# Hybrid attention layer: differential query and key projections accumulated side by side, with their weights loaded tile by tile

## Chip, cores and metric

The kernel runs on one core of a Trainium2 chip, in one launch. The metric is the device time of one execution in microseconds (us); lower is better. The times are medians over repeated executions.

## The reference

One layer (DEPTH 1) on x of 256 tokens by 1024 features, all float32. One input projection feeds two attention branches; cut to what matters:

```python
h = rms_norm(x, norm_g)
proj = einsum('bsd,de->bse', h, w_in)          # 1024 -> 4096, eight chunks of 512
mq, mk, mv, mg, dq, dk, dv, dg = split(proj)
# branch m: 8 heads of 64, causal softmax attention with ALiBi, all 256 keys in one block
mq, mk = rms_norm(mq, moba_q_norm), rms_norm(mk, moba_k_norm)
m_out = moba_attention(mq, mk, mv) * silu(mg)
# branch d: 4 heads, two softmax maps each
dq, dk = rms_norm(dq, diff_q_norm), rms_norm(dk, diff_k_norm)
a = softmax(q1 k1) - lam * softmax(q2 k2)
d_out = rms_norm(a @ dv, diff_subln) * 0.8 * silu(dg)
x = x + einsum('bse,ed->bsd', concat([m_out, d_out]), w_out)
```

## The kernel before

**The projections.** Every float32 product is made of three reduced-precision matmuls: each operand is split in a rounded part "hi" and the rest "lo", and hi·hi, hi·lo and lo·hi are accumulated (`PASSES`). x stands transposed in eight k tiles of 128 rows (`xhi`, `xlo`); the weights are split into `whi` and `wlo` in pieces of 1024 columns, two k tiles of one chunk each. A step `u.n` is one *unit*: one k tile (n % 8) of chunk n // 8 in the order of `CHUNKS` (dq, dk, dv, mq, mk, mv, dg, mg), which is six matmuls of 512 columns (three products for each of two token tiles). So `u.0` to `u.7` are dq, `u.8` to `u.15` are dk. Units from `u.64` on are the output projection.

**Splitting.** hi is a copy on ACT (ScalarE), lo a subtraction on DVE (VectorE). `x.k` splits x and dq's weights of k tile k (they come in one DMA, tile `first`); `h.i` and `l.i` make `whi` and `wlo` of piece i, from weight tiles `w` of 1 MB (two pieces each, step `L.j` loads tile j). Tile j lands in one of three buffers, the split pieces in one of six.

**Between the projections.** `sq`, `ssq`, `norm`, `sc` compute and apply the RMS factors of queries and keys (ACT and DVE). `T.dq`, `T.dk` transpose them on TensorE (PE), `Th` and `Tl` split them again (ACT, DVE). `S.d` are the scores of branch d, `post.dv` copies the values out of PSUM, `rcopy` copies a row of factors. `X`, `E`, `C` are the softmax (DVE, ACT, DVE or POOL), `AT`, `AC`, `AV` transpose the probabilities, copy them and multiply by the values. `gds`, `gdi`, `gdm` are the gate of branch d (ACT sigmoid, DVE, POOL), after which `T.d` transposes its output. Steps ending in m do the same for branch m.

**What sets the order.** The table `ORDER` is written out by hand: the program issues its steps one after another, so each engine runs its own instructions in the order of the table, and waits in place for what it needs. PSUM has eight banks, handed out by a first-in-first-out list (`bank`, `release`): a step can also wait for the reader of the bank that it is given. All loads and stores are issued by SP (SyncE) in table order; the loads of `small`, and of `first` for all eight k tiles, stand ahead of the table. The first tile comes in two halves, and the first unit works on halves of 256 columns.

**Warm-up.** `warm_up(N_WARM)` issues seven matmuls on zeros ahead of the first unit, `warm_up(N_FILL)` two more behind it. Each leaves two matmul records in the profile.

Of the kernel before, what the change touches and what calls it, by code (L numbers as in the profile page):

```python
# [22 lines left out]
MAGIC = float(0x5F1FFFF9)  # L23
N1, N2 = 0.703952253, 0.703952253 * 2.38924456
LAMBDA_INIT = 0.2
N_WARM, N_FILL, N_TILES = 7, 2, 9
OUT_ORDER = "dm"
CHUNKS = ["dq", "dk", "dv", "mq", "mk", "mv", "dg", "mg"]
GAIN = {"mq": 8, "mk": 9, "dq": 10, "dk": 11, "subln": 12}
# [5 lines left out]


ORDER = """
x.0 x.1 x.2 x.3 x.4 L.0 L.1 LX L.2 LL x.5 x.6 x.7 u.0 u.1 u.2 h.4 u.3 l.4 u.4 u.5 h.5 l.5 L.3 u.6 u.7 h.6 l.6 u.8
sq.dq h.7 u.9 ssq.dq l.7 L.4 xsq xst u.10 u.11 h.8 l.8 u.12 lsum u.13 rdiag u.14 h.9 l.9 L.5 u.15 lexp ldiff u.16
sq.dk ssq.dk h.10 h.11 l.10 norm.d l.11 L.6 u.17 sc.dq sc.dk u.18 u.19 rmm u.20 u.21 T.dq h.12 l.12 h.13 h.14 l.14  # L40
T.dk Th.dk Tl.dk l.13 L.7 u.22 Th.dq u.23 post.dv h.15 rcopy u.24 Tl.dq u.25 l.15 L.8 S.d X.d0 E.d0 u.26 X.d1 E.d1
X.d2 u.27 E.d2 X.d3 E.d3 u.28 C.d1 C.d0 u.29 h.16 l.16 u.30 C.d2 u.31 sq.mq h.17 l.17 L.9 AT.d0 AC.d0 u.32 C.d3
h.18 l.18 h.19 l.19 h.20 l.20 L.10 u.33 ssq.mq AV.d0 u.34 h.21 l.21 u.35 u.36 AT.d1 AC.d1 L.11 u.37 u.38 AV.d1
u.39 h.22 l.22 u.40 u.41 h.23 l.23 L.12 h.24 l.24 u.42 u.43 sq.mk ssq.mk sqd norm.m sc.mq sc.mk normd u.44 T.mk
Th.mk Tl.mk scd u.45 T.mq u.46 Th.mq Tl.mq h.25 l.25 L.13 u.47 post.mv u.48 h.26 h.27 l.26 l.27 h.28 L.14 u.49 S.m
h.29 u.50 u.51 X.m0 E.m0 l.28 u.52 C.m0 X.m1 X.m2 E.m1 C.m1 X.m3 u.53 h.30 l.29 L.15 u.54 E.m2 C.m2 E.m3 C.m3
AT.m0 AC.m0 u.55 gds l.30 u.56 gdi h.31 l.31 gdm L.16 u.57 u.58 AT.m1 AC.m1 AT.m2 AC.m2 u.59 h.32 l.32 h.33 u.60
T.d l.33 AT.m3 L.17 u.61 Th.d Tl.d h.34 u.62 AV.m2 AV.m1 AV.m0 l.34 AC.m3 AV.m3 u.63 gi.0 gi.1 h.35 u.64 l.35 u.65
u.66 gs.1 u.67 u.68 gs.0 u.69 u.70 gm.1 gh.1 gl.1 u.71 gm.0 gh.0 gl.0 h.36 l.36 h.37 l.37 u.72 h.38 l.38 h.39 l.39
u.73 u.74 u.75 u.79  # L50
""".split()


# [1 line left out]
def kernel(  # L55
# [45 lines left out]
    small = const.tile([P, 16 + S], F32, name="small")  # L101
    nc.sync.dma_start(out=small, in_=small_x)
    sm = small[:, 0:16]
    first = []
    for kt in range(KT):
        t = tile768("first")
        if kt == 0:
            for c in (slice(S, 512), slice(512, 768)):
                nc.sync.dma_start(out=t[:, c], in_=xw[kt][:, c])
        else:  # L110
            nc.sync.dma_start(out=t, in_=xw[kt])
        first.append(t)
    xn = const.tile([P, 2, D], F32, name="xn")

    def load_xn():
# [123 lines left out]
                                       op0=ALU.subtract, op1=ALU.subtract)  # L239


    raws, pieces = {}, {}

    def load_w(i):
        t = raw_pool.tile([P, 2048], F32, tag="raw", name=f"w{i}")
        n = 2 if i < 2 else 1
        for j in range(n):
            c = slice(j * 2048 // n, (j + 1) * 2048 // n)
            nc.sync.dma_start(out=t[:, c], in_=w[i][:, c])
        raws[i] = t  # L250
# [29 lines left out]
    def unit_nat(name, kt, piece):  # L280

        if kt == 0:
            acc[name] = [bank(f"acc_{name}{t}") for t in range(2)]
        wp = pieces[piece]
        n = 256 if name == CHUNKS[0] and kt == 0 else 512
        order = [(t, i, o) for t in range(2) for i in range(3) for o in range(0, 512, n)]
        if name == CHUNKS[0]:
            order.sort(key=lambda v: (v[2], (0, 2, 1)[v[1]]))
        for t, i, o in order:
            a, b = PASSES[i]  # L290
            c = (kt % 2) * 512 + o
# [321 lines left out]
    def unit_out(u, piece):  # L613
# [79 lines left out]
```

## Time and profile before

| | |
|---|---|
| time, median of 3 runs (lowest to highest) | 143.33 us (143.05 to 143.37) |
| time of the profiled execution | 143.47 us |
| its span on the core | 141.7 us |
| PE matmul busy | 137.4 us, 97% |
| DVE / ACT / POOL busy | 105.8 / 84.2 / 23.7 us |
| moved by DMA | 24.39 MB, mean 172 GB/s |

The span is what the profile covers; the 1.8 us between it and the time lie outside. Busy shares are means over stages with different limits, so the question is where PE waits, not how busy the others are. An instruction's printed length on PE is the time until its result is through the array; a stream of matmuls is counted by the distance between starts.

### The profile page before, as it was taken

To read this page: it belongs to the slowest core of one execution; us is meant where nothing else is said; L and a number is where in the kernel's file an instruction comes from. 1 tells how busy PE (TensorE), PEld (TensorE's weight loads), DVE (VectorE), ACT (ScalarE), POOL (GpSimd) and SP (SyncE) were. 2 spreads that over 40 slices of the span, in tenths; PEclk is the share of its full clock that TensorE was granted. 3 is DMA by queue.
4 is the path that set the end of the run, shared out by engine and by line. 5 is a ranking of instruction groups with operands and counts; after the bars stand their busy time and mean duration, and the time that the engine had idled before them with its cause. 6 is when DMAs were issued, how large, how long until landed. Compare 5 with 4: busy or idle time off the path is not lost.

```text
span 141.7 us, 2227 instructions
## 1 busy us (share of the span) xinstructions
PE 137.4 (97%) x806; PEld 116.8 (82%) x806; DVE 105.8 (75%) x249; ACT 84.2 (59%) x167; POOL 23.7 (17%) x28
## 2 busy tenths in 40 slices
PE   7999999999999999999999999999999999999990
PEld 7888878888888888888887888878999888898890
DVE  1699996889995998997799999994629435691331
ACT  4477894495192898955650599799768504660000
POOL 7980000000000000000000000279750007000000
PEclk9999999999999999999999999999999999999999
DMA  4999999670708700068960002925134900000232
GB/s 111 307 408 381 418 430 407 250 273 25 296 0 296 298 2 0 9 287 291 335 268 0 0 0 93 416 88 213 83 113 187 296 0 0 7 0 0 104 118 74
DMA packets 5482, 24.39 MB, mean 172 GB/s; under 512 B 608, under 2 KB 1376, under 8 KB 3424
## 3 DMA queue, kind: packets, MB, share of 16 engines
q1 hardware_dynamic: 5472, 24.26, 46.1%
q8 instruction: 6, 0.10, 0.3%
q14 instruction: 4, 0.03, 0.1%
HBM read 23.21 MB, written 1.05 MB: 171 GB/s over the span
## 4 chain that ended last, share of the span: by engine, by line
PE 94%; DMA 3%; SPq 1%; DVE 0%; ACT 0%; issue 0%
PE oacc L601 16%; PE acc_mg L307 8%; PE acc_mq L292 8%; PE acc_dg L292 8%; PE acc_mk L292 8%; PE acc_dv L292 8%; PE acc_mv L292 8%; PE acc_dk L292 8%; PE acc_dq L292 8%; PE s_ps L412 4%; PE T_ps L317 3%; DMA first<-xw 3%; PE mo_ps L494 2%; PE do_ps L500 1%; PE aT_ps L470 1%; PE aT_ps L472 1%
## 5 line engine op out<-in xcount | busy, mean ns | idle before, releaser
L276 DVE TENSOR_TENSOR wlo<-w,whi 128x1024 fp32r<-128x1024 f32 x36 | 43.3, 1231 | 6.1 <-ACT whi L272 5.9
L272 ACT ACTIVATE whi<-w 128x1024 fp32r<-128x1024 f32 x36 | 36.4, 1056 | 4.1 <-DVE nq L175 2.1
L442 POOL TENSOR_TENSOR p<-p,rs 128x512 f32<-128x512 f32 (+1 forms) x8 | 8.3, 1064 | 82.0 <-DVE rs L438 81.8
L432 ACT ACTIVATE p<-p,nmax 128x256 f32<-128x256 f32 (+1 forms) x32 | 14.1, 442 | 3.9 <-DVE nmax L422 3.9
L601 PE MATMUL oacc<-whi,mixm 128*128 128x512 f32 (+1 forms) x40 | 10.4, 347 | 0.0
L601 PE MATMUL oacc<-whi,mixd 128*128 128x512 f32 (+1 forms) x40 | 10.4, 346 | 0.0
L422 DVE CUSTOM_DVE_ANT_0 p<-s_ps,bias 128x256 f32<-128x256 f32 (+1 forms) x32 | 9.2, 352 | 1.6 <-PE s_ps L412 1.5
L307 PE MATMUL acc_mg<-xhi,whi 128*128 128x256 f32 x32 | 9.2, 289 | 0.0
L307 PE MATMUL acc_mg<-xhi,wlo 128*128 128x256 f32 x32 | 9.0, 281 | 0.0
L307 PE MATMUL acc_mg<-xlo,whi 128*128 128x256 f32 x32 | 9.0, 281 | 0.0
L608 DVE TENSOR_TENSOR o<-oacc,xn 128x512 f32<-128x512 f32 (+1 forms) x5 | 2.9, 585 | 7.7 <-PE oacc L601 7.7
L601 PEld LDWEIGHTS oacc<-whi,mixm 128*128 128x128 f32 x40 | 7.1, 189 | 1.0
L601 PEld LDWEIGHTS oacc<-whi,mixd 128*128 128x128 f32 x40 | 7.0, 188 | 1.0
L143 POOL TENSOR_SCALAR bias<-dist 128x256 f32<-128x256 f32 x8 | 7.6, 967 | 0.4
L264 ACT ACTIVATE whi<-first 128x512 fp32r<-128x512 f32 (+1 forms) x9 | 5.0, 578 | 3.5 <-DMA first<-xw 3.5
L601 PE MATMUL oacc<-wlo,mixd 128*128 128x512 f32 (+1 forms) x20 | 6.9, 347 | 0.0
L601 PE MATMUL oacc<-wlo,mixm 128*128 128x512 f32 (+1 forms) x20 | 6.9, 347 | 0.0
L265 DVE TENSOR_TENSOR wlo<-first,whi 128x512 fp32r<-128x512 f32 (+1 forms) x9 | 6.0, 663 | 1.2 <-ACT whi L264 1.2
L478 ACT ACTIVATE pT<-aT_ps 128x512 f32<-128x512 f32 x6 | 3.6, 593 | 5.4 <-PE aT_ps L471 5.4
L292 PE MATMUL acc_mk<-whi,xhi 128*128 128x512 f32 x16 | 6.7, 418 | 0.0
L292 PE MATMUL acc_dv<-whi,xhi 128*128 128x512 f32 x16 | 6.5, 408 | 0.0
L292 PE MATMUL acc_mv<-whi,xhi 128*128 128x512 f32 x16 | 6.5, 405 | 0.0
(167 smaller groups left out, 353.9 us busy)
## 6 DMA issues: line engine op xcount, KB each, us to landing
w<-w SPq DMA_DIRECT2D x16, 1024.0 KB, 4.9
first<-xw SPq DMA_DIRECT2D x7, 384.0 KB, 5.6
w<-w SPq DMA_DIRECT2D x4, 512.0 KB, 8.6
xn<-x SPq DMA_DIRECT2D x2, 512.0 KB, 9.6
out<-o SPq DMA_DIRECT2D x3, 256.0 KB, 2.1
first<-xw SPq DMA_DIRECT2D x2, 128.0 KB, 3.0
out<-o SPq DMA_DIRECT2D x2, 128.0 KB, 1.9
small<-small_x SPq DMA_DIRECT2D x1, 136.0 KB, 2.2
```

What stands on the lines that cost most here:

```text
L143: nc.gpsimd.tensor_scalar(out=b, in0=dist, scalar1=2.0 ** -(h + 1), scalar2=None, op0=ALU.mult)
L264: nc.scalar.activation(out=hi[:, c], in_=src, func=AF.Copy)
L265: nc.vector.tensor_tensor(out=lo[:, c], in0=src, in1=hi[:, c].bitcast(F32), op=ALU.subtract)
L272: nc.scalar.activation(out=piece(i)[0], in_=raw_half(i), func=AF.Copy)
L276: nc.vector.tensor_tensor(out=lo, in0=raw_half(i), in1=hi.bitcast(F32), op=ALU.subtract)
L292: nc.tensor.matmul(acc[name][t][:, o:o + n], lhsT=(xhi, xlo)[a][:, kt, t * P:(t + 1) * P], rhs=wp[b][:, c:c + n], start=kt == 0 and i == 0 ...
L307: nc.tensor.matmul(acc[name][j // 2][:, (j % 2) * S:(j % 2 + 1) * S], lhsT=wp[b][:, c:c + P], rhs=(xhi, xlo)[a][:, kt], start=kt == 0 and ...
L412: nc.tensor.matmul(ps[c][k][:, o:o + n], lhsT=qk[g + "q"][a][rows, pr, q0:q0 + P], rhs=qk[g + "k"][b][rows, pr, 0:n], start=i == 0, stop=i ...
L422: nc.vector.tensor_tensor_reduce(out=p[:, o:o + n], in0=s_ps[g][c][k][:, b:b + n], in1=biases[c][:, S - n:], scale=-1.0, scalar=3.0e38, op ...
L432: nc.scalar.activation(out=p[:, o:o + n], in_=p[:, o:o + n], func=AF.Exp, scale=-1.0, bias=mx[:, i:i + 1], accum_out=sums[g, pr][:, i:i + 1])
L442: nc.gpsimd.tensor_tensor(out=p3, in0=p3, in1=q.unsqueeze(2).to_broadcast([P, 2, n]), op=ALU.mult)
L601: nc.tensor.matmul(acc["o", c][j][:, 0:n], lhsT=qk[g][a][:, kt, t * P:(t + 1) * P], rhs=pieces[piece][b][:, o:o + n], start=first and i == ...
```

## The change

dq and dk are accumulated side by side: the units run `u.0 u.8 u.1 u.9 ... u.7 u.15`, in four PSUM banks. dk's weights, which came in four DMAs of 512 KB behind all of x and dq's weights, now come in eight DMAs of 256 KB, each right behind the tile `first` of its k tile. A new step `y.k` splits dk's weights of k tile k (512 columns instead of a piece of 1024). dk's matmuls take dq's sequence of products. One filling warm-up matmul behind the first unit is left out. The whole table of steps stands in a new order.

```diff
-N_WARM, N_FILL, N_TILES = 7, 2, 9
+N_WARM, N_FILL, N_TILES = 7, 1, 9
...
-x.0 x.1 x.2 x.3 x.4 L.0 L.1 LX L.2 LL x.5 x.6 x.7 u.0 u.1 u.2 h.4 u.3 l.4 u.4 u.5 h.5 l.5 L.3 u.6 u.7 h.6 l.6 u.8
+x.0 y.0 LX L.2 LL x.1 y.1 x.2 u.0 y.2 u.8 x.3 u.1 y.3 u.9 x.4 u.2 y.4 L.3 u.10 x.5 u.3 y.5 u.11 x.6 u.4 y.6 u.12
...
-    first = []
+    first, raws = [], {}
     for kt in range(KT):
         t = tile768("first")
         if kt == 0:
...
             nc.sync.dma_start(out=t, in_=xw[kt])
         first.append(t)
+        i, c = kt // 4, slice(kt % 4 * 512, kt % 4 * 512 + 512)
+        if kt % 4 == 0:
+            raws[i] = raw_pool.tile([P, 2048], F32, tag="raw", name=f"w{i}")
+        nc.sync.dma_start(out=raws[i][:, c], in_=w[i][:, c])
...
     def load_w(i):
-        t = raw_pool.tile([P, 2048], F32, tag="raw", name=f"w{i}")
-        n = 2 if i < 2 else 1
-        for j in range(n):
-            c = slice(j * 2048 // n, (j + 1) * 2048 // n)
-            nc.sync.dma_start(out=t[:, c], in_=w[i][:, c])
-        raws[i] = t
+        raws[i] = raw_pool.tile([P, 2048], F32, tag="raw", name=f"w{i}")
+        nc.sync.dma_start(out=raws[i], in_=w[i])
...
+    def split_second(kt):
+        hi, lo = piece(4 + kt // 2)
+        src, c = raws[kt // 4][:, kt % 4 * 512:kt % 4 * 512 + 512], slice(kt % 2 * 512, kt % 2 * 512 + 512)
+        nc.scalar.activation(out=hi[:, c], in_=src, func=AF.Copy)
+        nc.vector.tensor_tensor(out=lo[:, c], in0=src, in1=hi[:, c].bitcast(F32), op=ALU.subtract)
...
-        if name == CHUNKS[0]:
+        if name in CHUNKS[0:2]:
             order.sort(key=lambda v: (v[2], (0, 2, 1)[v[1]]))
```

**First place: PE behind the first unit.** Each row is a matmul in the program's order; `acc_dq` and `acc_dk` are the accumulators of the two token tiles. Before:

```order
12 L292 MATMUL acc_dq_197<-wlo,xhi 128x256
13 L292 MATMUL acc_dq_198<-wlo,xhi 128x256
14 L130 MATMUL warm_ps<-const-float32-0.0 128x128 x2
15 L292 MATMUL acc_dq_197<-whi,xhi 128x512
16 L292 MATMUL acc_dq_198<-whi,xhi 128x512
17 L292 MATMUL acc_dq_197<-whi,xlo 128x512
```

Now:

```order
12 L299 MATMUL acc_dq_183<-wlo,xhi 128x256
13 L299 MATMUL acc_dq_184<-wlo,xhi 128x256
14 L135 MATMUL warm_ps<-const-float32-0.0 128x128
15 L299 MATMUL acc_dk_202<-whi,xhi 128x512
16 L299 MATMUL acc_dk_203<-whi,xhi 128x512
17 L299 MATMUL acc_dk_202<-whi,xlo 128x512
18 L299 MATMUL acc_dk_203<-whi,xlo 128x512
19 L299 MATMUL acc_dk_202<-wlo,xhi 128x512
20 L299 MATMUL acc_dk_203<-wlo,xhi 128x512
21 L299 MATMUL acc_dq_183<-whi,xhi 128x512
```

A filling matmul is gone, and dk's unit of the first k tile stands where dq's second k tile stood, which comes one unit later.

**Second place: SP's first loads.** `first` and `w_80` are the tiles of x with dq's weights, and of dk's weights. Before:

```order
1 L102 DMA small<-small_x 128x272
2 L109 DMA first<-xw 128x256 x2
3 L111 DMA first<-xw 128x768 x7
4 L249 DMA w_172<-w 128x1024 x2
5 L249 DMA w_175<-w 128x1024 x2
```

Now:

```order
1 L102 DMA small<-small_x 128x272
2 L110 DMA first<-xw 128x256 x2
3 L117 DMA w_80<-w 128x512
4 L112 DMA first<-xw 128x768
5 L117 DMA w_80<-w 128x512
6 L112 DMA first<-xw 128x768
```

The load behind the first tile's second half is now dk's tile of 256 KB instead of the second tile of 384 KB, and the two kinds alternate.

**Third place: ACT between the transposes T.dq, T.dk and the scores S.d.** `dq`, `dk` are the split copies Th, `whi` the copies h, `dv` is post.dv, `rrow` is rcopy. Before:

```order
21 L272 ACTIVATE whi<-w_251 128x1024 x2
22 L272 ACTIVATE whi<-w_294 128x1024 x2
23 L272 ACTIVATE whi<-w_364 128x1024
24 L380 ACTIVATE dk<-T_ps,small 128x4x128 x2
25 L380 ACTIVATE dq<-T_ps,small 128x4x128 x2
26 L396 ACTIVATE dv<-acc_dv_374,r 128x512
27 L396 ACTIVATE dv<-acc_dv_375,r 128x512
28 L272 ACTIVATE whi<-w_364 128x1024
29 L217 ACTIVATE rrow<-r_ps 128x256
```

Now:

```order
28 L279 ACTIVATE whi<-w_244 128x1024 x2
29 L240 ACTIVATE lexp<-lsum 128x2
30 L387 ACTIVATE dq<-T_ps,small 128x4x128 x2
31 L279 ACTIVATE whi<-w_304 128x1024
32 L387 ACTIVATE dk<-T_ps,small 128x4x128 x2
33 L279 ACTIVATE whi<-w_304 128x1024
34 L279 ACTIVATE whi<-w_362 128x1024 x2
35 L403 ACTIVATE dv<-acc_dv_396,r 128x512
36 L403 ACTIVATE dv<-acc_dv_397,r 128x512
37 L222 ACTIVATE rrow<-r_ps 128x256
```

Both copies of `w_294` and one of `w_364` stood ahead of the split copies, the other of `w_364` behind `dv`. Now these four weight copies (`w_304`, `w_362` in the new numbers) stand between the first split copy and `dv`, where none did.

## Rows read from the trace of the kernel before

**Rows 1.** The chain that ended last, shares of the span by engine.

```profile
PE 94%; DMA 3%; SPq 1%; DVE 0%; ACT 0%; issue 0%
```

**Rows 2.** Busy time by stretch: stretch, its length, busy PE, PEld, DVE, ACT, POOL, clock, DMA, GB/s.

```profile
2.00:4.50 2.50, 2.50 (x12) 2.27 (x12) 1.47 (x3) 0.62 (x2) 2.41 (x4) 1.00 0.84 219
...
7.15:17.04 9.89, 9.89 (x46) 7.91 (x44) 9.79 (x19) 7.79 (x12) 2.84 (x3) 1.00 1.02 401
...
44.32:116.00 71.68, 71.68 (x490) 61.92 (x490) 56.42 (x158) 49.33 (x113) 11.86 (x10) 1.00 0.43 158
```

**Rows 3.** Waits of the weight-load side of PE, whole span: total, times, longest.

```profile
PEld acc_dq L292 <- ACT whi L264: 0.6, 2, 0.4
```

**Rows 4.** The chain in order of time, around the first units: start, length, what.

```profile
6.95 0.44 PE warm_ps L130 x4
7.39 9.81 PE acc_dq L292 x42
```

**Rows 5.** PE in order of time: start, length, what.

```profile
5.75 0.73 PE L292 MATMUL acc_dq<-whi,xhi 128*128 128x256 f32 x2
...
6.79 0.60 PE L130 MATMUL warm_ps<-const-float32-0.0 128*128 128x128 f32 x4
```

**Rows 6.** ACT in order of time, first conversions; in brackets the idle time before.

```profile
3.56 0.42 ACT L264 ACTIVATE whi<-first 128x256 fp32r<-128x256 f32 x1 [1.34 <-DMA first<-xw]
5.28 0.42 ACT L264 ACTIVATE whi<-first 128x256 fp32r<-128x256 f32 x1 [1.31 <-DMA first<-xw]
6.28 0.63 ACT L264 ACTIVATE whi<-first 128x512 fp32r<-128x512 f32 x1 [0.59 <-DMA first<-xw]
```

**Rows 7.** DVE in order of time, one subtraction of 512 columns.

```profile
8.68 0.68 DVE L265 TENSOR_TENSOR wlo<-first,whi 128x512 fp32r<-128x512 f32 x1
```

**Rows 8.** DVE in order of time, start and end of the normalization of dq and dk.

```profile
31.16 0.36 DVE L349 TENSOR_SCALAR m<-ss,r 128x16 f32<-128x16 f32 x2
...
35.89 1.28 DVE L359 TENSOR_TENSOR qn<-acc_dk,f 128x512 f32<-128x512 f32 x2
```

**Rows 9.** PE in order of time: transposes and scores of branch d, transposes of mk.

```profile
36.87 1.91 PE L317 MATMUL T_ps<-ident,qn 128*128 128x128 f32 x16
...
44.32 2.97 PE L412 MATMUL s_ps<-dk,dq 64*128 64x256 f32 x48
...
77.95 1.04 PE L317 MATMUL T_ps<-ident,qn 128*128 128x128 f32 x8
```

**Rows 10.** ACT in order of time, split copies and their neighbours.

```profile
38.38 1.27 ACT L380 ACTIVATE dk<-T_ps,small 128x512 fp32r<-128x512 f32 x2 [4.46 <-PE T_ps L317]
39.54 1.27 ACT L380 ACTIVATE dq<-T_ps,small 128x512 fp32r<-128x512 f32 x2
...
42.21 1.05 ACT L272 ACTIVATE whi<-w 128x1024 fp32r<-128x1024 f32 x1
43.16 0.37 ACT L217 ACTIVATE rrow<-r_ps 128x256 f32<-128x256 f32 x1
...
78.58 1.27 ACT L380 ACTIVATE mk<-T_ps,small 128x512 fp32r<-128x512 f32 x2 [5.87 <-PE T_ps L317]
```

**Rows 11.** The copies of dv: shortest, median and longest in ns, first and last start.

```profile
L396 ACT ACTIVATE dv<-acc_dv,r x2: 692/692/692, 40.9 to 41.6; 128x512 f32<-128x512 f32 x2
```

**Rows 12.** ACT in order of time, last exponentials of branch m and what follows.

```profile
95.81 0.49 ACT L432 ACTIVATE p<-p,nmax 128x256 f32<-128x256 f32 x1
...
97.56 0.57 ACT L478 ACTIVATE pT<-aT_ps 128x512 f32<-128x512 f32 x1
...
98.42 1.28 ACT L581 ACT_TABLE_LOAD   x1
```

**Rows 13.** PE in order of time: probabilities of branch m, output of branch d.

```profile
96.79 0.27 PE L470 MATMUL aT_ps<-ident,p 128*128 128x128 f32 x1
...
107.25 1.03 PE L317 MATMUL T_ps<-ident,dn 128*128 128x128 f32 x8
```

**Rows 14.** POOL in order of time, the gate multiplications of branch d.

```profile
101.27 3.51 POOL L591 TENSOR_TENSOR dn<-dn,sg 128x512 f32<-128x512 f32 x2 [0.82 <-DVE sg L585]
```

More of the change, by code (lines that the diff above doesn't have):

```diff
@@ L37 @@
 ORDER = """
-x.0 x.1 x.2 x.3 x.4 L.0 L.1 LX L.2 LL x.5 x.6 x.7 u.0 u.1 u.2 h.4 u.3 l.4 u.4 u.5 h.5 l.5 L.3 u.6 u.7 h.6 l.6 u.8
[L39 to L47, printed above, removed]
@@ L48 @@
-T.d l.33 AT.m3 L.17 u.61 Th.d Tl.d h.34 u.62 AV.m2 AV.m1 AV.m0 l.34 AC.m3 AV.m3 u.63 gi.0 gi.1 h.35 u.64 l.35 u.65
-u.66 gs.1 u.67 u.68 gs.0 u.69 u.70 gm.1 gh.1 gl.1 u.71 gm.0 gh.0 gl.0 h.36 l.36 h.37 l.37 u.72 h.38 l.38 h.39 l.39
-u.73 u.74 u.75 u.79
+x.0 y.0 LX L.2 LL x.1 y.1 x.2 u.0 y.2 u.8 x.3 u.1 y.3 u.9 x.4 u.2 y.4 L.3 u.10 x.5 u.3 y.5 u.11 x.6 u.4 y.6 u.12
+x.7 u.5 y.7 L.4 xsq xst rdiag h.8 l.8 u.13 u.6 lsum u.14 h.9 l.9 L.5 u.7 sq.dq ssq.dq u.15 sq.dk ssq.dk h.10 h.11
+l.10 u.16 rmm norm.d sc.dq sc.dk u.17 l.11 L.6 lexp ldiff u.18 u.19 u.20 u.21 T.dq Th.dq Tl.dq h.12 l.12 T.dk
@@ new lines @@
+Th.dk Tl.dk u.22 h.13 l.13 L.7 h.14 l.14 h.15 u.23 post.dv u.24 rcopy u.25 l.15 L.8 S.d X.d0 E.d0 u.26 X.d1 E.d1
+X.d2 E.d2 X.d3 u.27 u.28 C.d0 E.d3 C.d1 h.16 l.16 u.29 u.30 h.17 l.17 L.9 u.31 sq.mq AT.d0 AC.d0 C.d2 u.32 h.18
+l.18 h.19 l.19 h.20 l.20 h.21 l.21 L.10 u.33 C.d3 AV.d0 ssq.mq u.34 u.35 u.36 L.11 u.37 h.22 l.22 AT.d1 AC.d1 u.38
+u.39 u.40 u.41 AV.d1 h.23 l.23 L.12 h.24 l.24 u.42 u.43 sq.mk u.44 ssq.mk sqd norm.m sc.mq sc.mk normd T.mk Th.mk
+Tl.mk u.45 T.mq scd u.46 Th.mq Tl.mq u.47 post.mv h.25 l.25 L.13 h.26 h.27 l.26 h.28 l.27 h.29 u.48 L.14 u.49 S.m
@@ L51 @@
+u.50 X.m0 E.m0 u.51 l.28 u.52 C.m0 u.53 X.m1 X.m2 E.m1 X.m3 C.m1 l.29 L.15 E.m2 C.m2 u.54 AT.m0 AC.m0 E.m3 C.m3
+u.55 gds h.30 u.56 gdi h.31 l.30 l.31 L.16 u.57 u.58 AT.m2 AT.m1 AC.m1 u.59 gdm AC.m2 u.60 T.d h.32 h.33 h.34 l.33
+h.35 l.32 l.34 L.17 u.61 Th.d Tl.d AT.m3 u.62 AV.m0 l.35 AV.m2 AV.m1 AC.m3 AV.m3 u.63 gi.0 u.64 gi.1 gs.0 u.65
+gs.1 u.66 u.67 u.68 u.69 u.70 gm.1 gh.1 gl.1 u.71 gm.0 gh.0 gl.0 h.36 l.36 u.72 h.37 l.37 h.38 l.38 h.39 l.39 u.73
+u.74 u.75 u.79
 """.split()
@@ L239, in lam_diff @@
                                        op0=ALU.subtract, op1=ALU.subtract)
-    raws, pieces = {}, {}
+    pieces = {}
     def load_w(i):
-        t = raw_pool.tile([P, 2048], F32, tag="raw", name=f"w{i}")
-        n = 2 if i < 2 else 1
-        for j in range(n):
-            c = slice(j * 2048 // n, (j + 1) * 2048 // n)
-            nc.sync.dma_start(out=t[:, c], in_=w[i][:, c])
-        raws[i] = t
+        raws[i] = raw_pool.tile([P, 2048], F32, tag="raw", name=f"w{i}")
+        nc.sync.dma_start(out=raws[i], in_=w[i])
     def piece(i):
@@ L638 @@
     of_pair = {"X": maxima, "E": exps, "C": combine, "AT": probs_T, "AC": probs_copy, "AV": attend}
-    of_number = {"L": load_w, "x": split_first, "h": split_hi, "l": split_lo, "gi": gate_m_in, "gs": gate_m_sig,
+    of_number = {"L": load_w, "x": split_first, "y": split_second, "h": split_hi, "l": split_lo, "gi": gate_m_in, "gs": gate_m_sig,
                  "gm": gate_m_mul, "gh": gate_m_hi, "gl": gate_m_lo}
```

## The prediction

> **What bounds the kernel now.** I began with the chain of work that ended last: 94% of the span is PE, 3% DMA, and no other engine has a full percent [rows 1]. So the question is only where PE waits. The waits answer it: PE's weight loads waited for data twice in the whole span, 0.6 us in all, the longest 0.4 [rows 3]. Both lie in the first unit. The busy time by stretch says the same: from 7.15 us to 17.04 PE is busy for all 9.89 us, and from 44.32 to 116.00 for all 71.68 [rows 2]. A change that moves work in there gains nothing, however much it relieves ACT, DVE or the DMA queues. It can lose, if something that was ready in time no longer is. What can be gained lies ahead of 7.15 us. There the order of time shows the first unit's second half beginning at 5.75, just after ACT has converted the weights (5.28 + 0.42), which waited 1.31 us for their DMA; behind it stand four records of filling warm-up from 6.79 [rows 5, 6].
>
> **One filling matmul less.** The four warm-up records of the two filling matmuls take 0.44 us of the chain, 0.11 each [rows 4]. Two records go: **-0.22 us**, if what comes next is ready. PE is then free for it at 6.79 + 0.22 = 7.01 [rows 5].
>
> **dk's first tile as the next thing.** What comes next is now `u.8`, which needs dk's first 256 KB, where x's and dq's second 384 KB landed before. That one landed 1.00 us behind the second half of the first tile (6.28 against 5.28) [rows 6]. From below: at 401 GB/s, the rate from 7.15 on, 262 thousand bytes take 0.65 us. From above: at 219 GB/s, the rate from 2.0 to 4.5, they take 1.20 [rows 2]. So the tile lands between 5.93 and 6.48; with 0.63 for the conversion [rows 6] and 0.05 for the hand-over (5.70 to 5.75) `u.8` can begin between 6.61 and 7.16. I take the lower part, since the nearest row carried more bytes in 1.00 us: it is ready before 7.01, and the cost is 0. At the upper end it is +0.15.
>
> **The pairs behind it.** 42 matmuls of dq take 9.81 us [rows 4], 0.234 each, 1.40 a unit, and all units of 512 columns are alike. Side by side, a k tile keeps PE for 2 x 1.40 = 2.80 us, where it kept it for 1.40. It needs 384 + 256 KB, 1.63 us at 401 GB/s, so the loads run ahead of PE by more than a microsecond a tile. DVE has one subtraction of 0.68 us [rows 7] more in each of these 2.80, where it has long been keeping up with one k tile every 1.40; the total is what it was, since the same columns were subtracted later. I set this part at 0. The 14 further units of dq and dk take the same PE time in either order, and dk's last unit ends where it did.
>
> **The normalization.** dq's sums of squares used to be taken while dk ran; now both follow at the end. The group from the factors' first instruction to the last scaling began at 31.16; dq's two scalings were over when dk's began, at 35.89 [rows 8], and dq's transposes followed at 36.87 [rows 9]. Now the group begins a little later, because dq's reductions stand ahead of dk's and dk's two token tiles finish together. Even half a microsecond later dq's scalings are over at 36.4, ahead of PE at 36.87 - 0.22 = 36.65, and one weight subtraction has moved out of the group besides. Cost 0; without that cover each 0.1 would count in full, since PE's next rows are the transposes.
>
> **ACT ahead of the scores: a new wait.** This is the place where a term of the sum can turn up. `S.d` writes banks that hold `dv`'s accumulators until ACT has copied them (`post.dv`); before, they were copied straight behind the split copies. Now four weight copies stand between. PE's side: from the first transpose at 36.87 to the scores at 44.32 it has 7.45 us of work [rows 9]. ACT's side: 0.63 from the first transpose to the first split copy (77.95 to 78.58) [rows 9, 10]; 1.16 for each pair of split copies (38.38 to 39.54); 0.95 for each weight copy (42.21 to 43.16) [rows 10]; 0.69 for the first half of dv [rows 11]; 0.05 for the hand-over. Sum: 0.63 + 2 x 1.16 + 4 x 0.95 + 0.69 + 0.05 = 7.49. The wait is **+0.04**. From below it is 0. From above, with the printed lengths instead of the distances (1.27 and 1.05), the sum is 8.11 and the wait 0.66. I take the distances, since ACT runs these in a stream. Queued behind the waiting matmul are all the scores and the mq units, so a wait here goes into the end time in full.
>
> **The rest of the new order.** On PE, `AV.d1` moves behind two more units, `AT.m1` and `AT.m2` change places, `AT.m3` moves behind `u.61`: the same work, no gap of its own. Of the moves on the other engines one comes near PE: the last four exponentials of branch m now run behind the copy of `AT.m0`'s result instead of ahead of it. They began at 95.81, and the copy at 97.56, ahead of the table load at 98.42 [rows 12]. Now the copy follows the transposes (96.79 - 0.18, and 0.63 until a copy can begin, as above: 97.24) [rows 13] and takes 0.86 until the next instruction [rows 12], so the exponentials begin at about 98.10, 2.29 later; since the copy no longer follows them, the gate is 1.4 later. Its two POOL products, 101.27 + 3.51 [rows 14], end at about 106.2 instead of 104.78. `T.d` begins at 107.25 - 0.18 = 107.07 and reads the second product four transposes later [rows 13]. Almost a microsecond is left. Cost 0; a slower POOL would have to use that up first.
>
> **Sum.** -0.22 + 0 + 0.04 = -0.18 us. The profiled execution took 143.47, so it would take 143.29; the median of the runs is 143.33, so I predict 143.15. That is 0.13%: about 0.2%, 0.29 us here, is what a measurement of this kernel can tell from no change.
>
> **Rivals.**
>
> *The first tile lands earlier (faster).* Its two halves landed 1.72 us apart (3.56 and 5.28) [rows 6], though 128 KB take 0.60 even at 219 GB/s [rows 2]: the second half seems to share the engines with the tiles queued behind it. There 256 KB stand now instead of 384. PE waited up to 0.4 there [rows 3], so at most another 0.4 is gained: 142.75. From 0.11 on, it decides for faster. Against it: nothing in the profile says how the sharing goes.
>
> *ACT's chain holds up the scores (slower).* The upper sum above: 143.15 + 0.62 = 143.77. It decides for slower once the chain is longer than 7.45 by 0.51 us. For it: the margin in my sum is nothing. Against: in the rows, neighbouring ACT instructions overlap by 0.1 each.
>
> *dk's first tile is late (slower or the same).* At the upper bound +0.15, 143.30. It takes a landing at 6.8 or later, past every row, to make it slower by 0.29.
>
> *Loads do not keep up with two tiles a k tile (slower).* If each tile took 1.72 us, the longest distance in the rows, two would take 3.44 against PE's 2.80, 0.64 short in each of seven k tiles: 4.5 us, 147.6. Against it: 384 KB came in 1.00 us. A rule of the Trainium skill would favour this rival: the page "DMA: Bandwidth & Descriptors", section "Bandwidth", advises to batch transfers to 1 MiB or more for three quarters of the peak, and this change cuts 512 KB into 256. It was measured on the other issue path, and the row of 1.00 us for 384 KB, with many transfers in flight, speaks against it.
>
> *The projection side by side does nothing.* That is nearly my forecast: what I count comes from the filling matmul and the scores, not from the pairing.
>
> **How the numbers follow.** The forecast, within 0.2%: 0.48. The first tile earlier, or no wait at the scores together with some of it: 0.30. ACT's chain: 0.12. A late first tile or another wait of the new order: 0.08. Loads that don't keep up: 0.02. So faster 0.30, same 0.48, slower 0.22. The range goes from the first rival's end, 142.75, to the second's, 143.8; the 4.5 us case and a wait that I have overlooked are left out.
>
> **What would show it.** In the profile after: dk's first matmul at about 7.0, behind two warm-up records; no wait on PE between there and the transposes; the transposes at about 36.65; the scores at about 44.1 to 44.2, with ACT's copies of dv ending just there; `T.d` at about 107.1 without a wait on POOL. I would be wrong if PE's first matmul of `u.8` waits for ACT, if the second half of the first tile begins away from 5.75, or if the scores wait by several tenths.

## The result, and the profile after

The changed kernel takes 144.14 us (144.01 to 144.28, 6 runs), the kernel before 143.13 in the runs beside it (143.04 to 143.37, 6 runs). The ratio is 1.0067, with a 95% interval of 1.0054 to 1.0080: slower, by 1.0 us. The forecast was 143.15 with a range of 142.75 to 143.8, so it missed in sign and the range did not hold the time. Times and ratios are of fast executions; one execution of the kernel with an early touch below, 147.38 us, ran slow and is left out.

The chain of work that ended last, start, length, what. It answers to [rows 4] and, further down, to [rows 9, 13].

```profile
2.08 4.73 DMA w<-w
6.83 0.64 ACT whi L272
7.51 1.67 PE acc_dk L299 x6
...
28.89 1.40 PE acc_dv L299 x6
...
37.53 1.75 PE T_ps L324 x16
...
44.88 2.93 PE s_ps L419 x48
...
116.70 22.14 PE oacc L608 x120
...
138.86 0.42 DVE o L615
```

The same chain of the kernel before, at three of these places (new rows of the profile that the prediction used):

```profile
28.40 5.60 PE acc_dv L292 x24
...
37.04 1.75 PE T_ps L317 x16
...
138.30 0.42 DVE o L608
```

Read downwards: dv's first unit begins 0.49 later (28.89 against 28.40), the transposes 0.49 later (37.53 against 37.04), the last instruction 0.56 later (138.86 against 138.30). So 0.49 of the loss arises ahead of 28 us, and everything behind it, where most of the steps moved, adds 0.07. At its head the chain now runs through a DMA and a conversion: the load `w<-w` is dk's first tile, and `whi L272` is its conversion on ACT.

ACT in order of time, the first conversions; in brackets the idle time before and what ended it. It answers to [rows 6].

```profile
3.36 0.42 ACT L265 ACTIVATE whi<-first 128x256 fp32r<-128x256 f32 x1 [1.15 <-DMA first<-xw]
3.95 0.42 ACT L265 ACTIVATE whi<-first 128x256 fp32r<-128x256 f32 x1 [0.17 <-DMA first<-xw]
6.83 0.63 ACT L272 ACTIVATE whi<-w 128x512 fp32r<-128x512 f32 x1 [2.47 <-DMA w<-w]
```

The two halves of the first tile are converted from 3.36 and 3.95 on. Then ACT waits 2.47 us for dk's first tile. I had put its landing between 5.93 and 6.48; it was there at 6.82.

PE in order of time, around the end of the first unit, the transposes and the scores, and `T.d` (answers to [rows 5, 9, 13]):

```profile
6.06 0.38 PE L135 MATMUL warm_ps<-const-float32-0.0 128*128 128x128 f32 x2
7.51 0.73 PE L299 MATMUL acc_dk<-whi,xhi 128*128 128x512 f32 x2 [1.06 <-ACT whi L272]
...
37.37 1.91 PE L324 MATMUL T_ps<-ident,qn 128*128 128x128 f32 x16
...
44.81 1.40 PE L419 MATMUL s_ps<-dk,dq 64*128 64x256 f32 x20
...
107.77 1.03 PE L324 MATMUL T_ps<-ident,dn 128*128 128x128 f32 x8
```

The waits, by engine and line: us in total, times, longest (answers to [rows 3]):

```profile
ACT whi L272 <- DMA w<-w: 2.9, 2, 2.5
PEld acc_dk L299 <- ACT whi L272: 1.3, 1, 1.3
PE acc_dk L299 <- ACT whi L272: 1.1, 1, 1.1
PEld s_ps L419 <- ACT dv L403: 0.4, 1, 0.4
```

PE had no wait for data over 0.4 before; now it has one of 1.1, ahead of dk's first matmul. Its cause shows in the busy time by stretch. First the changed kernel (the columns are those of [rows 2], the last one GB/s):

```profile
4.00:6.00 2.00, 2.00 (x13) 2.00 (x13) 0.66 (x2) 0.36 (x1) 1.86 (x3) 1.00 0.78 131
7.15:17.04 9.89, 9.53 (x40) 7.54 (x41) 9.44 (x19) 7.48 (x14) 2.59 (x3) 1.00 1.04 396
```

Then the kernel before:

```profile
4.00:6.00 2.00, 1.93 (x8) 1.61 (x8) 0.84 (x3) 0.42 (x1) 1.86 (x3) 1.00 0.88 305
```

In the two microseconds from 4 to 6 the DMA engines were busy for 0.78 of the time (0.88 before), yet they moved 131 GB/s where they moved 305. They were not idle; they took longer for the same bytes. From 7.15 on the changed kernel runs at 396, against 401 before [rows 2].

### The profile page after: what moved, and what is told of

Same layout as the page of the kernel before. It is cut to its first block, busy times and chain, and to the rows that moved or that the text cites. A ratio compares the mean times of both kernels' runs of the same rounds, so it can differ in the third digit from the quotient of the medians.

```text
span 142.2 us, 2241 instructions
## 1 busy us (share of the span) xinstructions
PE 137.0 (96%) x804; PEld 116.5 (82%) x804; DVE 106.5 (75%) x253; ACT 84.5 (59%) x171; POOL 22.1 (16%) x28
## 4 chain that ended last, share of the span: by engine, by line
PE 92%; DMA 3%; SPq 1%; ACT 0%; DVE 0%; issue 0%
PE oacc L608 16%; PE acc_mg L314 8%; PE acc_dk L299 8%; PE acc_dg L299 8%; PE acc_mq L299 8%; PE acc_mk L299 8%; PE acc_mv L299 8%; PE acc_dv L299 8%; PE acc_dq L299 7%; PE s_ps L419 4%; DMA w<-w 3%; PE T_ps L324 3%; PE mo_ps L501 2%; PE do_ps L507 1%; PE aT_ps L479 1%; PE aT_ps L477 1%
## 5 line engine op out<-in xcount | busy, mean ns | idle before, releaser
L283 DVE TENSOR_TENSOR wlo<-w,whi 128x1024 fp32r<-128x1024 f32 x32 | 39.3, 1267 | 4.1 <-ACT whi L279 3.8
L279 ACT ACTIVATE whi<-w 128x1024 fp32r<-128x1024 f32 x32 | 31.7, 1058 | 2.7 <-DVE nq L180 2.0
L449 POOL TENSOR_TENSOR p<-p,rs 128x512 f32<-128x512 f32 (+1 forms) x8 | 7.3, 937 | 85.5 <-DVE rs L445 85.5
L273 DVE TENSOR_TENSOR wlo<-w,whi 128x512 fp32r<-128x512 f32 x8 | 5.5, 685 | 2.7 <-ACT whi L272 2.7
L272 ACT ACTIVATE whi<-w 128x512 fp32r<-128x512 f32 x8 | 5.0, 627 | 3.1 <-DMA w<-w 2.9
```

The lines of the kernel that those rows point to most:

```text
L279: nc.scalar.activation(out=piece(i)[0], in_=raw_half(i), func=AF.Copy)
L283: nc.vector.tensor_tensor(out=lo, in0=raw_half(i), in1=hi.bitcast(F32), op=ALU.subtract)
L449: nc.gpsimd.tensor_tensor(out=p3, in0=p3, in1=q.unsqueeze(2).to_broadcast([P, 2, n]), op=ALU.mult)
```

## The experiments

### The late tile: does it go away if dk comes later?

Edit: all of dk's loads and units one k tile behind dq's (the load of dk's tile k stands behind x's tile k + 1).

```diff
-x.0 y.0 LX L.2 LL x.1 y.1 x.2 u.0 y.2 u.8 x.3 u.1 y.3 u.9 ...
+x.0 x.1 y.0 LX L.2 LL x.2 y.1 u.0 u.1 u.8 x.3 y.2 u.2 u.9 ...
+        if kt:
+            load_dk(kt - 1)
+    load_dk(KT - 1)
```

> The changed kernel, but dk runs one k tile behind: loads x0, x1, dk0, x2, dk1 and so on, units u.0 u.1 u.8 u.2 u.9 and so on. Same work. In the changed kernel PE stood still for about 1.2 us before its first dk matmul, until dk's first tile had landed (6.82) and was converted. Theory 1, the tile stands too early in the queue, wherever it lies: now dk has 1.4 us more, the second load is again x's contiguous 384 KB, which landed at 6.28 before, so PE's wait falls to 0.3 or less and the time to 143.0 to 143.4. Theory 2, reads of w are slow by themselves and slow whatever stands near them: PE's wait stays above 0.8 in all, now partly before u.8 and partly before u.2, time 143.8 or more.

Measured: 143.79 us, ratio 1.0050 (1.0034 to 1.0066). x's second tile, which now stood behind the first, was converted at 6.47, PE waited 0.70 for it, and dk's first tile followed at 8.32; by the starts PE lost another 0.35 ahead of dk's first matmul (8.19 + 0.47 to 9.01). That is the second of the two theories, in time and wait. Busy time by stretch, the changed kernel from 5 to 7 us, then this one:

```profile
5.00:7.00 2.00, 1.45 (x11) 1.25 (x9) 0.00 (x0) 0.17 (x1) 1.85 (x3) 1.00 0.93 264
```

```profile
4.00:6.00 2.00, 2.00 (x13) 2.00 (x13) 0.63 (x2) 0.33 (x1) 1.86 (x3) 1.00 0.82 222
5.00:7.00 2.00, 1.46 (x11) 1.27 (x9) 0.49 (x2) 0.53 (x1) 1.86 (x3) 1.00 0.85 156
```

From 4 to 6 us the loads moved 222 GB/s instead of 131, from 5 to 7 us 156 instead of 264: the slow stretch moved back with dk's first tiles. So it belongs to them. Whether x's second tile was slowed as well is not shown: it was converted at 6.47, in the kernel before at 6.28 [rows 6] and, in two further profiles below, at 6.18 and (with one filling matmul less) at 5.42.

### The same bytes in other places

dk's tile of one k tile is 128 pieces of 2 KB (one for each partition). In the tensor `w` the pieces lie 8 KB apart, since a row holds four k tiles. x's tiles are pieces of 3 KB without gaps (only the two halves of the first one are pieces of 1 KB, 3 KB apart), and dk's tiles of the kernel before were pieces of 4 KB at 8 KB. In the next three kernels the bytes, the number of loads and their order are those of the changed kernel.

Edit of the first: dk's tiles without gaps, in a tensor of their own.

```diff
-        nc.sync.dma_start(out=raws[i][:, c], in_=w[i][:, c])
+        nc.sync.dma_start(out=raws[i][:, c], in_=wk[kt])
...
+    "wk": col["dk"].reshape(KT, P, 512)
```

> The changed kernel with dk's eight tiles in a tensor of their own, each 256 KB without gaps, instead of rows of 2 KB that lie 8 KB apart. Same transfers, same order. If the distance of the rows makes the first dk tile slow, it lands near 6.0 and the time falls by 0.7 or more, to 143.4 or less. If the first read of a region that nothing has read before is slow, or the place in the queue, it stays within 0.3 us of the changed kernel, 143.9 to 144.3.

Measured: 142.64 us, ratio 0.9964 (0.9944 to 0.9983): faster than both kernels. ACT's row of dk's first tile, PE's first matmul of dk, and the rate:

```profile
5.24 0.63 ACT L273 ACTIVATE whi<-w 128x512 fp32r<-128x512 f32 x1 [0.97 <-DMA w<-wk]
```

```profile
5.67 0.38 PE L136 MATMUL warm_ps<-const-float32-0.0 128*128 128x128 f32 x2
5.92 0.73 PE L300 MATMUL acc_dk<-whi,xhi 128*128 128x512 f32 x2
```

```profile
4.00:6.00 2.00, 2.00 (x16) 1.94 (x15) 1.00 (x4) 0.90 (x2) 1.86 (x3) 1.00 0.98 322
```

The tile is converted 1.59 us earlier (5.24 against 6.83), and PE takes it without a wait, behind the filling matmul. Of the 1.59 by which dk's first matmul begins earlier (7.51 to 5.92) 1.35 arrives at the end: the last instruction begins at 137.51 instead of 138.86. The other 0.24, net, is given back at a new place. The waits and the chain of this kernel show it:

```profile
PEld acc_dv L300 <- DVE wlo L284: 0.4, 1, 0.4
```

```profile
12.73 8.63 DMA xn<-x
21.38 1.35 ACT junk L194 x4
...
36.75 1.14 DVE wlo L284
37.94 2.83 PE acc_dv L300 x11
```

x's rows (`xn`) land at 21.38, their squares and the normalization follow on ACT and DVE, and a weight subtraction queued behind the last scaling (36.75 + 1.14) is what dv's projection now waits for. In the changed kernel PE's late start covered this chain: there the same subtraction ended at 37.21 + 1.22 = 38.43, and the matmul that needs it began at 39.36.

Edit of the second: the same tiles without gaps, but at their old place inside `w`.

```diff
-        nc.sync.dma_start(out=raws[i][:, c], in_=w[i][:, c])
+        dk = w.rearrange("i p n -> i (p n)")[i][kt % 4 * P * 512:(kt % 4 + 1) * P * 512]
+        nc.sync.dma_start(out=raws[i][:, c], in_=dk.rearrange("(p n) -> p n", n=512))
...
+    pieces[0] = col["dk"].reshape(2, P, 2048)
```

> The changed kernel with dk's weights at the same place in the same tensor w, only ordered so that each 256 KB tile lies without gaps. If the run without gaps was fast for the gaps alone, this is as fast as the one with a tensor of its own: 142.4 to 142.9, first dk tile landed by 5.5. If the tensor w itself, or its place in memory, is slow to read at first, it stays at 143.7 or more.

Measured: 142.83 us, ratio 0.9990 (0.9973 to 1.0008); dk's first conversion began at 5.05 and dk's first matmul followed without a wait, at 6.22. So the place inside `w` is not the reason. The tile came a little earlier here than in the tensor of its own, but PE's first unit was slower in the profiled execution, so dk began 0.30 later.

Edit of the third: dk's 2 KB behind x's 3 KB in the same rows of 5 KB, so both tiles have gaps.

```diff
+                nc.sync.dma_start(out=t, in_=xw[kt][:, 0:768])
...
+        nc.sync.dma_start(out=raws[i][:, c], in_=xw[kt][:, 768:1280])
```

> The changed kernel with dk's tiles behind x and dq's weights in the same rows (rows of 5 KB, of which 3 KB and 2 KB are read by separate transfers). Same transfers, same order, and dk's first tile lies in the rows that the first tile's two halves have just read. If the first read of a region is slow, dk's first tile lands 0.7 us or more earlier and the time falls to 143.4 or less. If the distance of rows is what is slow (5 KB now), or the place in the queue, it stays at 143.9 or more.

Measured: 143.06 us, ratio 0.9995 (0.9978 to 1.0011); the conversion began at 5.68, dk's first matmul at 6.37, without a wait. Gaps alone don't do it. By itself this run would also fit a slow first read, since x had just been read from the same rows; but the tensor of the first layout had not been read before either, and was fast.

### Is it the first touch?

Edit: the changed kernel, with an early load of 512 bytes of every row of dk's first rows, issued by ACT.

```diff
+    touch = const.tile([P, 128], F32, name="touch")
+    nc.scalar.dma_start(out=touch, in_=w[0][:, 0:128])
```

> The changed kernel with one more small load, issued by ACT ahead of everything: 512 bytes of each of the 128 rows of dk's first weight tile, into a tile that nobody reads. Nothing else. If the slow stretch from 3.5 to 6 us (78 to 205 GB/s) comes from the first read of these rows, wherever they lie, the touch takes the slowness upon itself ahead of the other loads and the time falls by 0.5 us or more, to 143.6 or less. If it comes from 2 KB pieces that lie 8 KB apart, however often they were read, the time stays at 143.9 or more.

Measured: 144.48 us, ratio 1.0097 (1.0078 to 1.0116). The stretch from 4 to 6 us ran at 142 GB/s, dk's first conversion began at 7.26. The touch was issued at 0.71 and landed 2.7 us later, ahead of that stretch, but behind the issue of dk's first load (2.10). So a part of every row read shortly before helped nothing; a touch that is over before dk's first load is issued was not tried. In this execution the second half of the first tile was late too (converted at 5.32, PE waited 0.63 for it), so the rate says more here than the time.

### Which distance?

Four kernels read dk's pieces of 2 KB from a tensor of their own, at another distance each; nothing else differs. The edits: a row of 2048 numbers (8 KB), of 2048 + 64 (8 KB + 256 bytes), of 1024 (4 KB), of 4096 (16 KB).

```diff
-        nc.sync.dma_start(out=raws[i][:, c], in_=w[i][:, c])
+        nc.sync.dma_start(out=raws[i][:, c], in_=wk[i][:, c])
```

> dk's weights in a tensor of their own, as pieces of 2 KB in rows of 8 KB and 256 bytes, so that the distance of the pieces is no power of two. If gaps as such make the first transfers slow, dk's first tile still lands at about 6.8, PE waits 1 us ahead of dk's first matmul, and the time is 144.1. If the slowness hangs on the distance of exactly 8 KB, the tile lands at 5.0 to 5.7 and the time is 142.6 to 142.9.

> dk's weights in a tensor of their own, as pieces of 2 KB at a distance of 4 KB: gaps half as wide. If the slowness grows with the width of the gaps, the tile lands between 5.3 (no gaps) and 6.8 (gaps of 6 KB), at about 6, and the time lies between 142.6 and 144.1. If any gap does it, landing and time are those of the changed kernel; if only 8 KB does, 142.7.

> dk's weights in a tensor of their own, as pieces of 2 KB in rows of exactly 8 KB. If the distance of 8 KB is what makes the first transfers slow, dk's first tile lands at about 6.8 and the time is that of the changed kernel, 144.1. If it is the place in the large tensor, the tile lands at 5.0 to 5.7 and the time is 142.6 to 143.2, as with rows of 8 KB and 256 bytes.

> dk's weights in a tensor of their own, as pieces of 2 KB in rows of 16 KB. If powers of two from 8 KB on are slow at the beginning, the tile lands at 6.8 or later and the time is 144.1 or more. If only the large tensor matters, 142.6 to 143.2.

The changed kernel ran once more beside the last two.

> The changed kernel, unaltered. If the late tile belongs to the kernel and not to one execution, dk's first tile lands at about 6.8 again, PE waits about 1 us for it and the time is 144.1. If it was the luck of the profiled execution, the tile lands at about 5.5 and the loss would have to come from elsewhere.

PE's first matmul of dk in this second profile:

```profile
7.80 0.73 PE L299 MATMUL acc_dk<-whi,xhi 128*128 128x512 f32 x2 [1.19 <-ACT whi L272]
```

All layouts together, in the order of the rate. The rate is that of the stretch from 4 to 6 us and, like the starts of ACT's first conversion of dk and of PE's first matmul of dk, from one profiled execution each; the time is the median.

| pieces of dk's tile | GB/s, 4 to 6 us | dk's conversion begins, us | dk's first matmul, us | time, us | ratio (95%) |
|---|---|---|---|---|---|
| in `w`, 8 KB apart (changed kernel) | 131 | 6.83 | 7.51 | 144.14 | 1.0067 (1.0054 to 1.0080) |
| the same again | 142 | 7.12 | 7.80 | 144.31 | 1.0078 (1.0058 to 1.0097) |
| own tensor, 8 KB apart | 156 | 6.48 | 7.16 | 143.89 | 1.0052 (1.0035 to 1.0069) |
| own tensor, 16 KB apart | 198 | 5.89 | 6.57 | 143.28 | 1.0014 (0.9995 to 1.0034) |
| own tensor, 4 KB apart | 274 | 5.92 | 6.60 | 143.02 | 0.9996 (0.9979 to 1.0012) |
| own tensor, 8 KB + 256 bytes apart | 303 | 5.23 | 5.91 | 143.18 | 0.9998 (0.9977 to 1.0018) |
| own tensor, no gaps | 322 | 5.24 | 5.92 | 142.64 | 0.9964 (0.9944 to 0.9983) |
| in rows with x, 5 KB apart | 339 | 5.68 | 6.37 | 143.06 | 0.9995 (0.9978 to 1.0011) |
| in `w`, no gaps | 395 | 5.05 | 6.22 | 142.83 | 0.9990 (0.9973 to 1.0008) |

PE's row at dk's first matmul, in the kernel with its own tensor at 8 KB:

```profile
7.16 0.73 PE L300 MATMUL acc_dk<-whi,xhi 128*128 128x512 f32 x2 [1.09 <-ACT whi L273]
```

and in the one with 256 bytes more:

```profile
5.91 0.74 PE L300 MATMUL acc_dk<-whi,xhi 128*128 128x512 f32 x2
```

256 bytes between the rows decide. At exactly 8 KB the first transfers are slow in either tensor and the kernel is slower; at 8 KB + 256 bytes they are not. 16 KB and 4 KB lie between: dk's first conversion begins at 5.89 and 5.92, and PE waits 0.51 and 0.72 for it; at 16 KB neither of the two cases expected came. So it is not the width of the gap (16 KB has the widest) and not any power of two alike. The profiled execution with the padded rows was the fastest of its ten (142.51, median 143.18), so its 5.23 is rather early (the one at exactly 8 KB, 6.48, was the fastest of its six as well, 143.65); the verdict rests on the two ratios, whose intervals are far apart. The time follows dk's first matmul: up to about 6.6 nothing is lost against the kernel before, whose second k tile begins at 7.15 [rows 2] and, in a second profile below, at 6.87. What the layouts with gaps at 4 KB, 5 KB and 8 KB + 256 bytes lose against the one without, some 0.4 to 0.5 us, is not settled: at 4 and 5 KB dk's first matmul comes 0.68 and 0.45 later, with the padded rows it does not, and the tile in `w` without gaps has an interval that meets theirs.

### The filling matmul by itself

Edit: the kernel before, with one filling matmul less and nothing else; and the layout without gaps, with none at all.

```diff
-N_WARM, N_FILL, N_TILES = 7, 2, 9
+N_WARM, N_FILL, N_TILES = 7, 1, 9
```

```diff
-N_WARM, N_FILL, N_TILES = 7, 1, 9
+N_WARM, N_FILL, N_TILES = 7, 0, 9
```

> The kernel before with one filling matmul instead of two, nothing else. My sum counted 0.22 us for it. If PE's second unit was free to start then (its weights were converted at 6.91, PE free at 7.01), the time falls by 0.15 to 0.25, to about 142.9. If the filling matmul stood in a wait for data in most executions, the time doesn't change.

> dk's tiles without gaps, and no filling warm-up matmul. If the filling matmul stands on the path wherever dk's first tile is there ahead of PE, the time is 0.15 to 0.22 us below that of the layout alone (142.64), about 142.45. If in most executions the next conversion is what PE waits for, the two are the same within 0.1.

Measured: 143.13 us for the first, ratio 1.0008 (0.9986 to 1.0030); the 0.22 us of the forecast would be 0.9985, just outside the interval. For the second 142.86 us, ratio 0.9974 (0.9960 to 0.9988), beside 0.9964 with the filling matmul. Neither shows a gain. To see why, the kernel before was profiled a second time.

> The kernel before, unchanged, for a second trace. The one that the prediction rests on took 143.47, above the median of 143.1. If the first loads differ from execution to execution, the second half of the first tile lands near 4 us here instead of 5.25, as in the run with one filling matmul, and the first dk unit or second dq unit begins 0.3 to 0.5 earlier; if not, the trace is as before within 0.1.

It took 143.31 us. ACT's rows at the start, then PE's:

```profile
6.18 0.63 ACT L264 ACTIVATE whi<-first 128x512 fp32r<-128x512 f32 x1 [1.91 <-DMA first<-xw]
```

```profile
3.85 0.79 PE L292 MATMUL acc_dq<-whi,xhi 128*128 128x256 f32 x2
4.44 0.63 PE L292 MATMUL acc_dq<-whi,xlo 128*128 128x256 f32 x2
...
6.51 0.61 PE L130 MATMUL warm_ps<-const-float32-0.0 128*128 128x128 f32 x4
6.87 0.73 PE L292 MATMUL acc_dq<-whi,xhi 128*128 128x512 f32 x2
```

The weights of the second k tile are ready at 6.18 + 0.63 = 6.81, and its first matmul starts at 6.87. With no filling matmul at all it could not start earlier than that: in this execution the filling stands in a wait for data. So it does in the profile of the layout without gaps, where dk's weights are ready at 5.24 + 0.63 = 5.87 and its first matmul begins at 5.92. It is not so in every execution. In the profile of the kernel with one filling matmul less (142.85 us, the fastest of its ten) the second k tile was converted by 5.42 + 0.63 = 6.05, ahead of PE:

```profile
6.44 0.38 PE L130 MATMUL warm_ps<-const-float32-0.0 128*128 128x128 f32 x2
6.58 0.71 PE L292 MATMUL acc_dq<-whi,xhi 128*128 128x512 f32 x2
```

There the filling matmul does stand on the path, for 0.14. The second look at the kernel before is also another start than that of [rows 5, 6]: there the second half of the first tile was converted at 5.28, here both halves were done by 4.28, and the second k tile's unit began at 6.87 instead of 7.15:

```profile
7.15 0.72 PE L292 MATMUL acc_dq<-whi,xhi 128*128 128x512 f32 x2
```

### Filling the new gap

Edit: the layout without gaps, and x's rows loaded ahead of the last two k tiles, so that the normalization could begin earlier; then the same with the squares of x placed ahead of the last k tile's copies on ACT; then that without a filling matmul.

```diff
+        if kt == 6:
+            load_xn()
```

```diff
-x.7 u.5 y.7 L.4 xsq xst rdiag h.8 l.8 ...
+xsq x.7 u.5 y.7 L.4 xst rdiag h.8 l.8 ...
```

> dk's tiles without gaps in their own tensor, and x's rows for the norm (xn, 1 MB) loaded ahead of the last two k tiles instead of behind all eight. In the run without gaps PE waited about 0.3 us at 37.6 for a weight subtraction that DVE does behind the normalization, which began when xn had landed (21.4). With xn about 3 us earlier and the k tiles still ahead of PE, that wait goes: 142.3, 0.3 under the run without gaps. If the last k tiles then come too late, PE waits near 23 to 26 us and the time is 142.8 or more.

> As the last run with x's rows loaded ahead of the last two k tiles, but the squares of x stand ahead of the last k tile's copies on ACT. If that place is why the run missed, the normalization begins earlier, the wait of 0.9 us at dv's projection goes and the time is at most that of the contiguous layout alone, 142.4 to 142.65. If delaying the last two k tiles is what hurt, the last unit of dq still waits and the time stays near 143.8.

> As the run before, without any filling warm-up matmul. If a filling matmul stands on the path wherever the next tile is there in time (dk's first tile lands at about 5.2, ahead of PE), this saves the two records of 0.11 us, so 0.15 to 0.22 us against the run before. If PE's clock or the next conversion sets the start of dk's first unit, the time is the same within 0.1.

Measured: 143.86 us (ratio 1.0054, 1.0034 to 1.0073), 144.23 (1.0077, 1.0057 to 1.0096) and 144.17 (1.0073, 1.0049 to 1.0098). All three missed, and gave back everything the layout had won. ACT's rows of the second one:

```profile
18.28 0.63 ACT L268 ACTIVATE whi<-first 128x512 fp32r<-128x512 f32 x1 [2.76 <-DMA first<-xw]
18.95 0.63 ACT L275 ACTIVATE whi<-w 128x512 fp32r<-128x512 f32 x1
19.49 0.62 ACT L196 ACTIVATE junk<-xn 128x512 f32<-128x512 f32 x1
...
21.95 0.49 ACT L161 ACTIVATE xhi<-first,small 128x256 fp32r<-128x256 f32 x1
```

and the waits that it ends in:

```profile
PEld acc_dv L302 <- DVE wlo L286: 0.9, 2, 0.6
PEld T_ps L327 <- DVE qn L369: 0.4, 2, 0.2
```

The megabyte of x's rows makes ACT wait 2.76 us for the seventh k tile, and the eighth is split at 21.95. DVE subtracts that tile's weights ahead of the factors in its own queue, so the normalization begins later, not earlier, whichever way ACT is ordered: the first scaling of dq began at 35.72, in the layout without gaps alone at 34.27. Those 1.45 are what the end loses: the last instruction begins at 138.96 instead of 137.51. The queue that had to be watched was DVE's. The filling matmul changed nothing here either (144.17 against 144.23), and the end hangs on this chain, not on PE's start.

## Why the prediction was wrong, point by point

**The step that failed.** "I take the lower part, since the nearest row carried more bytes in 1.00 us: it is ready before 7.01, and the cost is 0", with +0.15 at the upper end. Both ends came from rates of other tiles, 401 and 219 GB/s [rows 2], and the row of 1.00 us [rows 6] is x's tile, whose pieces have no gaps. I priced bytes and never asked where they lie in memory. With pieces 8 KB apart the start of the kernel ran at 131 GB/s, dk's first tile was there at 6.82, and its first matmul began at 7.51, 0.50 behind the 7.01 of the sum; in the second profile of the changed kernel at 7.80, 0.79 behind. That the layout does it is shown: the same kernel with the same loads and no gaps starts dk at 5.92 and takes 142.64. The rival "dk's first tile is late" named the mechanism and the point from which it decides, a landing at 6.8, but I had put it past every row and given it 0.08 together with any other wait of the new order.

**One filling matmul less, -0.22.** Not seen. The term rests on one execution: in another of the kernel before the next unit waits for its data at that place anyway, and without that matmul the kernel before gave 1.0008. It was also too large. By the distance between starts the four records take 0.36 [rows 2, 5], from 6.79 to 7.15, and where two of them stood on the path, they took 0.14 (6.44 to 6.58).

**The profiled execution of before.** I made the sum on it, 143.47 us, with the start of [rows 5, 6]. The second look at the same kernel begins the second k tile's unit 0.28 earlier, at 6.87. Against that start dk's first matmul is late by 0.64 in one profile of the changed kernel (7.51) and by 0.93 in the other (7.80); the last instruction begins 0.71 and 1.00 later (138.86 and 139.15 against 138.15), and the times of the three executions differ by 0.70 and 1.00 (144.01 and 144.31 against 143.31). So between these executions the late tile is nearly the whole loss, and the medians differ by 1.01.

**The pairs and the loads behind them, 0.** Right: from 7.15 to 17.04 the loads come at 396 GB/s, and each unit behind the first two takes 1.40. Tiles of 256 KB in place of 512 KB did not fall behind PE.

**The normalization, 0.** Right in the changed kernel: dq's scalings were over by about 36.1 (34.81 + 1.29), well ahead of the transposes, which the late start had put at 37.37, and dv's projection was not held up. With PE 1.59 earlier, in the layout without gaps, only 0.1 was left (34.27 + 1.29 = 35.56, the transposes at 35.66), and the subtraction queued behind the scalings cost 0.24. So the term came out right in part by luck: the wait for dk hid what stood behind it.

**ACT ahead of the scores, +0.04.** Right within what can be read. PE's rows have 44.81 - 37.37 = 7.44 from the transposes to the scores, where they had 7.45 [rows 9], and the chain has 7.35 in both kernels (37.53 to 44.88, and 37.04 to 44.39 before). ACT's copy of dv ends just there, as the sum of 7.49 had it (44.10 + 0.69 = 44.79), and the profile puts an idle of 0.4 on the weight-load side down to it; but the kernel before has the same 0.4 at this place without it, and the scores' matmuls begin no later. The prediction also counted two waits for data on the weight-load side in the whole span; there is a third of 0.4, ahead of branch m's scores, which both kernels have.

**The rest of the order, 0.** Right: `T.d` begins 0.52 later (107.77 against 107.25 [rows 13]), which is the 0.49 of the start, and waits for nothing on POOL, whose last product ended at 103.54 + 3.52 = 107.06. That is 0.86 behind the 106.2 of the sum, of which the late start explains 0.5, so less of the margin was left than I had reckoned.

**The first rival, an earlier first tile.** It landed earlier, at 3.95, but the second profile of before shows the same (both halves converted by 4.28), so the change need not have brought it, and what it gave was lost in the wait for dk.

A rule of the Trainium skill comes near the cause. The page "DMA: Bandwidth & Descriptors", section "Latency and other measured facts", says that copies between memory tensors slow down when the rows of a tile lie a large power of two apart, from 207 GB/s at 512 KiB to 103 at 4 MiB, and calls the reason behind it an inference. The runs here agree that an exact distance can matter and that padding cures it, but they differ in where: these are loads, not copies between memory tensors, the slowness is greatest at 8 KB, far below the page's distances, and smaller at 16 KB, it is seen only in the first tiles, and 256 bytes of padding were enough.

## What to carry to other kernels

A load's price is not its bytes over a rate of the same profile: ask what pieces it reads and how far apart they lie, above all for the first tiles, for which PE waits in full. When a weight is cut into smaller tiles, lay each tile out without gaps; here that turned a loss of 0.7% into a gain of 0.4% with the tiles in a tensor of their own; with the tiles in `w` the gain, 0.1%, is not clear of noise. And look at a second profile of the kernel before, before the sum is made: the first microseconds differ from execution to execution, and a term of 0.2 us that rests on them may stand in a wait.

## What the runs showed of the hardware

With pieces of 2 KB at a distance of 8 KB in the queue, the loads moved 131 to 156 GB/s in the stretch from 4 to 6 us, with the DMA engines busy for 0.6 to 0.9 of it, and 393 to 401 GB/s from 7.15 to 17.04, with nothing changed in their layout. Why only the first tiles are slow stays open; a touch of their rows a little earlier did not help.

The start of PE differs too. In the second profile of before, pairs of 256-column matmuls begin 0.43 apart from 4.44 until about 6.15; in the profile with padded rows they begin 0.24 apart from 4.33 on:

```profile
4.33 0.41 PE L300 MATMUL acc_dq<-whi,xlo 128*128 128x256 f32 x2
4.58 0.40 PE L300 MATMUL acc_dq<-wlo,xhi 128*128 128x256 f32 x2
```

The busy time by stretch gives the granted clock of that time (the third value from the right). The second profile of before:

```profile
3.50:5.00 1.50, 1.50 (x8) 1.44 (x8) 1.16 (x3) 0.71 (x2) 1.46 (x2) 1.00 0.82 279
```

The kernel with padded rows:

```profile
3.50:5.00 1.50, 1.50 (x11) 1.50 (x11) 1.08 (x3) 0.61 (x2) 1.44 (x3) 1.00 0.88 266
```

PE is busy throughout in both and the clock reads 1.00, the 2.4 GHz level, yet one has eight records of matmuls in 1.5 us and the other eleven. What ends the slower pace stays open. A first unit that is done up to a microsecond earlier or later would explain why kernels that wait for nothing at the start scatter more (142.28 to 143.19 without gaps) than the changed kernel, whose start hangs on a tile (144.01 to 144.28, and 144.10 to 144.51 the second time); that this is the reason was argued here, not tested.
